# Token-major branch gates and unsplit first blocks in a three-layer float32 network

## The chip, the cores and the metric

One core of a Trainium2 chip runs the whole program in one launch. The metric is the device time of that launch in microseconds (us); lower is better. The times shown are the median of several runs; one more execution was profiled, and every duration below is of that execution.

## What is computed

A sequence of 256 tokens with 2048 features goes through three layers in float32, one after the other.

```python
# first_block: attention, retention and memory branches, then
x = x + rms_norm(mixed @ w_out, g_post_mix)
h2 = rms_norm(x, g_pre_ffn)
f_gate, f_up = split(h2 @ w_ffn_in)                  # feed-forward
x = x + rms_norm((silu(f_gate) * f_up) @ w_ffn_out, g_post_ffn)
# second_block, layer 0: state-space mixer
h = modulate(rmsnorm(x, norm_g[0]), shift, scale)
u, z = split(h @ w_in)
...
x = x + gate * ((y * sigmoid(y @ w_glu + b_glu)) * silu(z) @ w_out)
# second_block, layer 1: attention with three branches
h_kv = modulate(rmsnorm(x, kv_norm_g), kv_shift, kv_scale)
kv = h_kv @ w_kv
proj = h @ w_qg                                      # queries, gates, z
o_br = stack([o_cmp, o_sel, o_win])
o = sum(gates * silu(z) * o_br)                      # over the 3 branches
x = x + gate * (o @ w_o)
out = rmsnorm(x, final_norm_g)
```

The precision has to be that of float32. The kernel gets it by writing each operand as a sum of two parts, hi and lo, of the type float32r, and adding three products: hi hi, hi lo and lo hi.

## The kernel before

**Weights.** A weight matrix is read in units of 2 contraction steps (of 128 rows) by 512 columns, 512 KB. `unit` (line 169) loads one into a tile `raw` (four buffers) from SP's queue and lets `split` (line 148) write `hi` by a cast on ACT (line 156) and `lo` by a subtraction (line 157) on DVE, or on POOL where an engine is given. Three buffers each hold `whi` and `wlo`.

**Products.** `ws` (line 190) makes a feature-major block: the weights are stationary, the 256 tokens move, 24 products of 256 columns a unit. `as_` (line 224) makes a token-major block: 128 tokens of the operand are stationary, 512 weight columns move, 12 products of 512 columns a unit. Both go over the units once and have both token halves in each. After each unit `pump` takes steps of side work (tables of the state-space layer, modulation vectors, attention) into the same queues. `do_late` runs steps that a block left for the middle of the next one.

**By halves.** Where a layer's output must be complete before the next layer's norm, the last block is made by token halves: `as_last` (line 277) keeps the split units in slots (`by_tokens`, line 254) and runs all units for tokens 0 to 127, then for 128 to 255, so that the first half's norm can run under the second half's products. `as_first` (line 301) does the same for the first block of the next layer: all units of the first half, then of the second, with split weights (eight units; subtractions on POOL by `shared=True`) and `ready(k, t)` called one unit ahead, which turns two feature blocks of half `t` on PE, scales them and splits them. The turning product multiplies by a diagonal of the reciprocal norms (`diags`, line 355), made by a chain of small DVE instructions (`rstd` and `rstds`, lines 326 to 374) behind sums of squares on ACT (`square`, line 343).

**The three first blocks.** The feed-forward's first block (line 915) is an `as_` with `ahead(ready)`, where `ready` is that of `post_norm` (line 842); the state-space layer (`ssm`, from line 1376) and the attention layer (`nsa`, from line 1696) call `as_first`, their operands made by `ssm_operand` (line 1345) and `nsa_operand` (line 1666). `hold` and `hold_act` put the splits of the first block's weights behind the first half's diagonal on DVE and the last square on ACT.

**The gate blocks.** In `nsa` each of four head groups makes three blocks of 512 columns of `w_qg` (one a branch) with `ws`, applies silu, multiplies by the branch's attention output, adds the branches up feature-major in `acc` and splits the sum into the operand `o`. `nsa_attention` makes the outputs feature-major, with one product of 512 columns (4 heads x 128 tokens) for a block of keys.

**The order of the work.** Each engine has one queue with a fixed order, found at build time by a scheduler that simulates the program; `issue_after(ins)` puts what is issued inside it behind `ins` on the engine of `ins`.

Of the kernel before, what the change touches and what calls it, by code (L numbers as in the profile page):

```python
# [64 lines left out]

class Slot:
# [7 lines left out]
class Kernel:  # L74
# [8 lines left out]
    def __init__(self, tc, a, out, ctx):  # L83
# [10 lines left out]
        self.hold = self.hold_act = None  # L94
# [74 lines left out]
    def unit(self, wv, k0, c0, n=512, j=None, place=None, engine=None):  # L169
# [9 lines left out]
        rows = wv[:, k0:k0 + 2] if len(wv.shape) == 3 else wv[:, k0 // 4, k0 % 4:k0 % 4 + 2]  # L179
        nc.sync.dma_start(raw[:, :, :n], rows[:, :, c0:c0 + n])  # L180
# [9 lines left out]
    def ws(self, act, wv, c0, j=None, before=None, quiet=False, shared=False):  # L190
# [6 lines left out]
        for k0 in range(0, nk, 2):  # L197
            if before is not None:
                before(k0)
            hi, lo = self.unit(wv, k0, c0, j=j, engine=self.nc.gpsimd if shared else None)  # L200
            for n in range(4):
                c = slice(n * 128, n * 128 + 128)
                for k in range(2):
                    self.mm3(ps[n // 2][:, n % 2], hi[:, k, c], lo[:, k, c], act, k0 + k,
                             start=k0 + k == 0 and n % 2 == 0, stop=k0 + k == nk - 1)
            if before is None and not quiet:
                self.pump()
        return ps
# [15 lines left out]
    def as_(self, act, wv, c0, before=None, quiet=False, shared=False):  # L224
# [6 lines left out]
        for k0 in range(0, nk, 2):  # L231
# [4 lines left out]
            hi, lo = self.unit(wv, k0, c0, engine=self.nc.gpsimd if shared else None)  # L236
# [17 lines left out]
    def by_tokens(self, units, products, shared=False, beside=None):  # L254

# [5 lines left out]
        for t in range(2):  # L261
            for u, (wv, k0, c0) in enumerate(units):
                if t == 0:
                    place = self.slot([128, 2, 2, 512], F32R, "kept") if u < len(units) - 3 else None
                    with self.tc.issue_after(self.hold) if self.hold else nullcontext(), \
                            self.tc.issue_after(self.hold_act) if self.hold_act else nullcontext():
                        kept.append((place, self.unit(wv, k0, c0, place=place,
                                                      engine=self.nc.gpsimd if shared else None)))
# [4 lines left out]
                if t and beside:  # L273
                    beside.popleft()()
# [26 lines left out]
    def as_first(self, act, wv, c0, ready):  # L301


        units = [(wv, k0, c0) for k0 in range(0, 16, 2)]
        ps = [self.mp.tile([128, 512], F32, name=f"mm{i}") for i in range(2)]

        def products(t, u, hi, lo):
            r = slice(t * 128, t * 128 + 128)
            if u == 0:
                ready(0, t)  # L310
            if u < 7:
                ready(u * 2 + 2, t)
            for k in range(2):
                kk = u * 2 + k
                xh, xl = act.hi(kk)[:, r], act.lo(kk)[:, r]
                self.mm(ps[t], xh, hi[:, k], kk == 0, False)
                self.mm(ps[t], xh, lo[:, k], False, False)
                self.mm(ps[t], xl, hi[:, k], False, kk == 15)

        self.by_tokens(units, products, True)  # L320
        self.hold = self.hold_act = None
        return ps
# [518 lines left out]
    def post_norm(self, act, w, g, x_src):  # L841
# [8 lines left out]
        h2 = Act(self, 0)  # L850
        r, beside = [], deque()
# [6 lines left out]
        def done(t, b, p):  # L858
            add(t, b, p)
            r.append(self.rstds(ss[:, t:t + 1]))  # L860
            if t == 0:
                for i in range(4):
                    normed(i, 0)
                for k in range(0, 16, 4):
                    beside.append(partial(both, k))
# [6 lines left out]
        def both(k):  # L872
            ready(k, 0)
            ready(k + 2, 0)

        def ready(k, t):

            while h2.n < k + 2:
                h2.grow()
            if t == 1 and k % 4 == 0:  # L880

                with self.tc.issue_after(self.last_scaled) if k else nullcontext():
                    normed(k // 4, 1)
            elif t == 1:
                with self.tc.issue_after(self.last_hi):
                    for i in range(2):
                        self.square(xs[i].t[:, k // 4 * 512:k // 4 * 512 + 512], new[:, i, k // 4:k // 4 + 1])
            p = self.ps([128, 2, 128], "tp", 2)
            rows = slice(t * 128, t * 128 + 128)
            for j in range(2):  # L890
                nc.tensor.transpose(p[:, j], xs[t].t[:, (k + j) * 128:(k + j) * 128 + 128], self.ident)
            for j in range(2):
                self.split(h2.hi(k + j)[:, rows], h2.lo(k + j)[:, rows], p[:, j], self.vec["g_pre_ffn"][:, k + j:k + j + 1])
# [10 lines left out]
        return xs, h2, partial(ready, t=1), new  # L904

    def ffn(self, xs, h2, ready, ss):
# [5 lines left out]
        for f0, f1 in ((0, 3), (3, 6), (6, 9), (9, 11)):  # L912
            s = Act(self, (f1 - f0) * 4)
            for f in range(f0, f1):
                ps = self.as_(h2, wi, f * 512, before=None if f else self.ahead(ready), shared=f == 0)
# [35 lines left out]
            for b in range(2 if last else 4):  # L951
                ps = self.as_(s, wo[:, f0 * 4:f1 * 4], b * 512)
# [9 lines left out]
        def done(t, b, p):  # L962
            with self.tc.issue_after(self.hold) if self.hold else nullcontext():
# [4 lines left out]
            for i in range(4):  # L968
# [3 lines left out]
                last_square = self.square(x, new[:, t, i:i + 1])  # L972
            ds.extend(self.diags(new[:, t:t + 1]))
            if t == 0:
                self.hold, self.hold_act = self.last_diag, last_square
                for k in range(0, 4, 2):
                    operand[1](k, 0)

        self.as_last(s, wo[:, 36:], (2, 3), done)
# [26 lines left out]
    def first(self):  # L1006
# [57 lines left out]
        xs, h2, ready, ss = self.post_norm(mx, a["w_out"], a["g_post_mix"], a["x"][0])  # L1064
# [3 lines left out]
        operand = self.ffn(xs, h2, ready, ss)  # L1068
# [278 lines left out]
    def ssm_operand(self, xs, ds):  # L1347
# [3 lines left out]
        h = Act(self, 0)  # L1351
        there = set()

        def ready(k, t):
# [3 lines left out]
            while h.n < k + 2:  # L1358
                h.grow()
            p = self.ps([128, 2, 128], "tp", 2)  # L1360
            w = self.work([128, 2, 128], "half")
# [3 lines left out]
            for j in range(2):  # L1365
                c = slice(k + j, k + j + 1)
# [623 lines left out]
```

## Time and profile before

| | us |
|---|---|
| median of 3 runs | 3202.23 |
| lowest, highest | 3200.45, 3205.97 |
| the profiled execution | 3202.57 |
| its span, first to last instruction | 3200.7 |

In the profile PE is the matmul part of TensorE, PEld its weight loads, DVE VectorE, ACT ScalarE, POOL GpSimd, SP the queue that issues most loads. A plain float32 product stands as two records, one of float32r as one. The granted clock of TensorE is given as a share of its full speed, and has two levels here, 1.00 (2.4 GHz) and 0.50 (1.2 GHz).

### The profile page before, as it was taken

What the parts mean: (1) busy time and instruction counts of PE and PEld (TensorE: products, weight loads), DVE (VectorE), ACT (ScalarE), POOL (GpSimd) and SP (SyncE); (2) the same over time, 40 slices, a digit from 0 to 9 for tenths busy, and PEclk for the clock granted to TensorE, in tenths of its full rate; (3) what the DMA queues carried; (4) which work ended last, traced back from release to release, by engine and by line L of the source; (5) the groups of instructions that cost most, each with busy time, mean ns of one, the idle gap of its engine ahead of it and who ended that gap; (6) DMA issues with size and microseconds to landing.
All of it is one profiled execution on the core that took longest, in us unless ns stands there. A gap on an engine that the chain in (4) does not pass through costs nothing. (4 is left out here: it accounts for less than half of the span.)

```text
span 3200.7 us, 48551 instructions
## 1 busy us (share of the span) xinstructions
PE 3108.7 (97%) x18694; PEld 2684.0 (84%) x18694; DVE 2344.8 (73%) x3580; ACT 1461.7 (46%) x2066; POOL 204.8 (6%) x296
## 2 busy tenths in 40 slices
PE   9999999999999998999999999799999899999998
PEld 8999888988888886877878778678898798999997
DVE  7777787767887766999989956656577865655656
ACT  5544444344444445444334355455444534444544
POOL 0000000000000002000000045400000200000000
PEclk9999999999999999999999999899999999999999
DMA  8868867888778874787777799388888585455575
GB/s 281 262 193 271 256 213 232 257 280 272 230 247 271 262 269 153 236 277 248 260 260 264 264 324 331 122 262 284 233 242 266 168 276 156 139 152 158 148 234 165
DMA packets 428040, 753.43 MB, mean 235 GB/s; under 512 B 31764, under 2 KB 90808, under 8 KB 426912
## 3 DMA queue, kind: packets, MB, share of 16 engines
q1 hardware_dynamic: 413520, 710.39, 69.6%
q0 software_dynamic: 13648, 38.88, 3.5%
q8 instruction: 146, 2.39, 0.3%
q10 hardware_dynamic: 640, 1.07, 0.1%
q14 instruction: 86, 0.70, 0.1%
HBM read 725.13 MB, written 33.49 MB: 237 GB/s over the span
## 5 line engine op out<-in xcount | busy, mean ns | idle before, releaser
L156 ACT CAST whi<-raw 128x1024 fp32r<-128x1024 f32 (+2 forms) x1059 | 1030.4, 982 | 1326.2 <-PE mm L150 1137.0
L157 DVE TENSOR_TENSOR wlo<-raw,whi 128x1024 fp32r<-128x1024 f32 (+2 forms) x1045 | 1178.2, 1136 | 585.0 <-ACT whi L156 574.3
L150 PE MATMUL mm<-whi,act 128*128 128x512 f32 x5072 | 1586.8, 392 | 6.4 <-ACT whi L156 5.6
L150 PEld LDWEIGHTS mm<-whi,act 128*128 128x128 f32 x5072 | 952.3, 188 | 214.8 <-issue 10.2
L150 PE MATMUL mm<-act,whi 128*128 128x256 f32 (+1 forms) x5440 | 1010.7, 287 | 3.9 <-ACT whi L156 3.8
L150 PE MATMUL mm<-wlo,act 128*128 128x512 f32 x2536 | 996.5, 393 | 13.8 <-DVE wlo L157 11.8
L150 PEld LDWEIGHTS mm<-act,whi 128*128 128x128 f32 (+1 forms) x5440 | 850.7, 192 | 27.2 <-issue 18.5
L150 PE MATMUL mm<-act,wlo 128*128 128x256 f32 (+1 forms) x2720 | 776.3, 288 | 2.5 <-DVE wlo L157 2.5
L150 PEld LDWEIGHTS mm<-wlo,act 128*128 128x128 f32 x2536 | 477.4, 188 | 125.4 <-DVE wlo L157 21.3
L150 PEld LDWEIGHTS mm<-act,wlo 128*128 128x128 f32 (+1 forms) x2720 | 519.2, 192 | 15.6 <-issue 10.1
L1097 DVE SCALAR_TENSOR_TENSOR acc<-side_raw,c_act,acc 128x512 f32<-128x512 f32 x480 | 359.2, 748 | 18.8 <-DMA side_raw<-mod_w 14.1
L150 PE MATMUL mm<-kept,act 128*128 128x512 f32 x360 | 93.1, 404 | 7.7 <-DVE act L157 7.7
L150 PEld LDWEIGHTS mm<-kept,act 128*128 128x128 f32 x360 | 68.3, 194 | 22.9 <-DVE act L157 8.8
L1117 POOL DMA_DIRECT2D mod<-side x24 | 12.0, 500 | 940.7 <-ACT side L1116 939.1
L1315 POOL DMA_DIRECT2D direct<-kern x128 | 66.9, 544 | 27.6 <-DMA direct<-kern 16.6
L1285 DVE TENSOR_TENSOR side<-tables,ssm_c 128x512 f32<-128x512 f32 x64 | 65.5, 1082 | 3.7 <-DMA ssm_c<-ssm_c_re 3.7
L150 PE MATMUL tp<-diag,x 128*128 128x128 f32 x192 | 32.0, 313 | 21.8 <-DVE diag L363 15.7
L150 PEld LDWEIGHTS tp<-diag,x 128*128 128x128 f32 x192 | 30.5, 224 | 26.2 <-issue 9.0
L156 ACT CAST kept<-raw 128x1024 fp32r<-128x1024 f32 x30 | 31.2, 1049 | 32.9 <-DMA raw<-w_out 8.2
L160 DVE SCALAR_TENSOR_TENSOR act<-tp,vec,act 128x256 fp32r<-128x256 f32 (+1 forms) x64 | 25.4, 412 | 22.1 <-ACT act L159 22.0
L157 DVE TENSOR_TENSOR kept<-raw,kept 128x1024 fp32r<-128x1024 f32 x20 | 24.5, 1225 | 21.0 <-ACT kept L156 20.8
L346 ACT ACTIVATE big<-x 128x512 f32<-128x512 f32 x40 | 25.1, 629 | 28.1 <-DVE x L1653 18.8
(390 smaller groups left out, 1889.5 us busy)
## 6 DMA issues: line engine op xcount, KB each, us to landing
raw<-w_in SPq DMA_DIRECT2D x272, 512.0 KB, 4.5
side_raw<-mod_w SPq DMA_DIRECT2D x192, 512.0 KB, 5.3
raw<-w_ffn_in SPq DMA_DIRECT2D x176, 512.0 KB, 5.3
raw<-nsa_w_qg SPq DMA_DIRECT2D x128, 512.0 KB, 3.7
raw<-w_ffn_out SPq DMA_DIRECT2D x88, 512.0 KB, 6.0
side_raw<-kv_mod_w SPq DMA_DIRECT2D x64, 512.0 KB, 4.7
raw<-ssm_w_in SPq DMA_DIRECT2D x64, 512.0 KB, 5.4
raw<-w_kv SPq DMA_DIRECT2D x48, 512.0 KB, 4.0
```

The source lines that it names most:

```text
L150: return self.nc.tensor.matmul(out, lhsT, rhs, start=start, stop=stop, skip_group_check=True).ins
L156: self.last_hi = nc.scalar.copy(hi, src).ins
L157: self.last = (engine or nc.vector).tensor_sub(lo, src, hi.bitcast(F32)).ins
L160: self.last_scaled = nc.vector.scalar_tensor_tensor(lo, src, scale, hi.bitcast(F32), op0=OP.mult, op1=OP.subtract).ins
L346: return self.nc.scalar.activation(self.work([128, 512], "big"), x, AF.Square, accum_out=out).ins
L1097: nc.vector.scalar_tensor_tensor(acc, raw[:, k], c, acc, op0=OP.mult, op1=OP.add)
L1117: nc.gpsimd.dma_start(flat[n:n + 4].rearrange("(o k) p -> o (k p)", o=1), row[r])
L1285: nc.vector.tensor_mul(w[i], y[r][:, :, :, None].to_broadcast([128, 4, 8, 16]), x[q][:, :, None, :].to_broadcast([128, 4, 8, 16]))
L1315: nc.gpsimd.dma_start(self.direct[g // 8, :, g % 8].rearrange("(c s) w -> c s w", s=8), src)
```

## The change

**Unsplit first blocks.** A class `Unsplit` holds an operand as plain float32 in two slots. The three `ready` functions write the scaled operand there and no longer split it. `as_first` takes the weights as they are loaded (six units in three slots, two in `raw` buffers), with one plain float32 product in place of three, and no weight is split. While the second half's products run, `rest(k)` splits the operand, two contraction steps of both halves at a time, for the later blocks. The feed-forward's first block becomes an `as_first` too; its first-half operand is made beside the second half of the last block of `post_norm`, as are two steps in the other two layers, by `beside(u)`.

**The queue behind the operand's splits.** When the fifth of these eight splits has been issued, `hold` remembers its two instructions, and the next `as_` issues the splits of its units 0 to 2 behind them. `hold_act` and the POOL engine for subtractions are gone. The feed-forward's last `as_` takes no side work.

**Token-major gates.** The twelve gate blocks use `as_`; the attention outputs are made token-major, four products of 128 columns for one of 512; the sum over branches is transposed and split for each group by `transpose_act`, as late work of the next block. `ws` runs late work after its second unit.

```diff
+class Unsplit:
+    def x(self, i):
+        while len(self.slots) <= i // 8:
+            self.slots.append(self.k.slot([128, 8, S], F32, "unsplit"))
+        return self.slots[i // 8].t[:, i % 8]
+    def rest(self, act):
+        def rest(k):
+            while act.n < k + 2:
+                act.grow()
+            self.k.split(act.hi(k, 2), act.lo(k, 2), self.slots[k // 8].t[:, k % 8:k % 8 + 2])
...
 ws:
+            if k0 == 2:
+                self.do_late()
...
 as_:
-            hi, lo = self.unit(wv, k0, c0, engine=self.nc.gpsimd if shared else None)
+            with ExitStack() as held:
+                for ins in self.hold:
+                    held.enter_context(self.tc.issue_after(ins))
+                hi, lo = self.unit(wv, k0, c0)
+            if k0 == 4:
+                self.hold = ()
...
-    def as_first(self, act, wv, c0, ready):
+    def as_first(self, x, wv, c0, ready, rest):
+        for t in range(2):
             r = slice(t * 128, t * 128 + 128)
+            ready(0, t)
+            for u in range(8):
+                k0 = u * 2
+                if u < 7:
+                    ready(k0 + 2, t)
+                if t == 0:
+                    if u < 6:
+                        if u % 2 == 0:
+                            slots.append(self.slot([128, 2, 2, 512], F32, "kept_raw"))
+                        raw = slots[-1].t[:, u % 2]
+                    else:
+                        raw = self.wp.tile([128, 2, 512], F32, name="raw", bufs=4)
+                    self.nc.sync.dma_start(raw, self.rows_of(wv, k0)[:, :, c0:c0 + 512])
+                    raws.append(raw)
+                for k in range(2):
+                    self.mm(ps[t], x(k0 + k)[:, r], raws[u][:, k], k0 + k == 0, k0 + k == 15)
+                if t:
+                    rest(k0)
+                    if u == 4:
+                        self.hold = self.last, self.last_hi
...
 post_norm:
+        def beside(u):
+            if u > 3:
+                ready(u * 2 - 8, 0)
...
 ffn:
-                ps = self.as_(h2, wi, f * 512, before=None if f else self.ahead(ready), shared=f == 0)
+                ps = self.as_(h2, wi, f * 512) if f else self.as_first(first[0], wi, 0, *first[1:])
...
-                ps = self.as_(s, wo[:, f0 * 4:f1 * 4], b * 512)
+                ps = self.as_(s, wo[:, f0 * 4:f1 * 4], b * 512, quiet=last and b == 1)
...
-            with self.tc.issue_after(self.hold) if self.hold else nullcontext():
+            with self.tc.issue_after(self.last_diag) if t else nullcontext():
                 add(t, b, p)
...
 nsa:
-                ps = self.ws(h, wq, D + 48 + br * D + g * 512)
+                ps = self.as_(h, wq, D + 48 + br * D + g * 512)
...
+            self.late += [partial(self.transpose_act, [acc[:, t] for t in range(2)], o, 4, g * 4, 0.5), self.Q[g].free]
...
 nsa_attention:
-                    self.mm(o.rearrange("p h t -> p (h t)"), self.vsw.t[:, br, m, g * 128:g * 128 + 128],
-                            pT.rearrange("p h t -> p (h t)"), m == 0, m == t)
+                    for h in range(4):
+                        self.mm(o[:, h], pT[:, h], self.vsw.t[:, br, m, g * 128:g * 128 + 128], m == 0 and h == 0, m == t)
```

## Rows read from the trace of the kernel before

**Rows 1.** The page, first part: busy us, share, instructions of each engine.
```profile
PE 3108.7 (97%) x18694; PEld 2684.0 (84%) x18694; DVE 2344.8 (73%) x3580; ACT 1461.7 (46%) x2066; POOL 204.8 (6%) x296
```

**Rows 2.** Stretches: from:to, length, busy per engine (instructions), PE clock, DMA share, GB/s.
```profile
1226.00:1261.00 35.00, 27.06 (x115) 19.30 (x114) 22.83 (x59) 20.16 (x52) 15.54 (x7) 0.95 0.42 119
2012.00:2070.00 58.00, 36.73 (x160) 31.05 (x161) 40.77 (x76) 27.14 (x55) 26.18 (x19) 0.76 0.29 88
2489.00:2507.00 18.00, 9.88 (x44) 7.48 (x43) 16.96 (x30) 7.93 (x18) 12.49 (x7) 0.81 0.77 253
2800.00:2840.00 40.00, 40.00 (x317) 37.98 (x315) 20.76 (x26) 20.06 (x29) 0.00 (x0) 1.00 0.54 158
```

**Rows 3.** Stretches of PE alone: from:to, length, busy, clock, DMA share, GB/s.
```profile
1237.09:1240.50 3.41, 3.41 (x9) 0.50 0.00 0
2015.33:2035.81 20.48, 9.63 (x36) 0.50 0.37 113
2046.05:2052.87 6.82, 4.92 (x17) 0.50 0.49 149
2500.02:2506.85 6.83, 3.07 (x10) 0.50 0.71 218
```

**Rows 4.** Timeline of PE from 2011: start, us, instruction, idle before and its releaser.
```profile
2011.51 0.39 PE L150 MATMUL mm<-whi,act 128*128 128x512 f32 x1
2020.52 2.05 PE L150 MATMUL tp<-diag,x 128*128 128x128 f32 x8 [8.63 <-DVE diag L363]
...
2047.95 2.07 PE L150 MATMUL tp<-diag,x 128*128 128x128 f32 x8 [7.09 <-DVE diag L363]
```

**Rows 5.** Timeline of DVE and POOL there, from the first half's last addition on.
```profile
2004.45 0.69 DVE L946 TENSOR_TENSOR y<-mm,y 128x512 f32<-128x512 f32 x1 [3.58 <-PE mm L150]
2013.46 2.17 POOL L1315 DMA_DIRECT2D direct<-kern  x4
2013.86 0.16 DVE L341 SCALAR_TENSOR_TENSOR bit<-bit 128x1 f32<-128x1 f32 x1
2014.06 6.32 DVE L363 TENSOR_SCALAR diag<-ident,bit 128x128 f32<-128x128 f32 x1
2015.53 4.75 POOL L157 TENSOR_TENSOR kept<-raw,kept 128x1024 fp32r<-128x1024 f32 x2
2506.21 0.28 DVE L363 TENSOR_SCALAR diag<-ident,bit 128x128 f32<-128x128 f32 x1
```

**Rows 6.** Line 157 on POOL: count, ns least, median and most, first and last start.
```profile
L157 POOL TENSOR_TENSOR wlo<-raw,whi x14: 2332/2390/2817, 1222.6 to 2500.2; 128x1024 fp32r<-128x1024 f32 x14
```

**Rows 7.** Timeline of PE: runs of equal products; x is how many a row merges.
```profile
1213.78 6.28 PE L150 MATMUL mm<-kept,act 128*128 128x512 f32 x27
...
1290.21 0.60 PE L807 MATMUL tp<-ident,big 128*128 128x128 f32 x4
...
2065.15 1.05 PE L150 MATMUL tp<-diag,x 128*128 128x128 f32 x8
...
2710.89 1.02 PE L150 MATMUL pv<-side,vsw 128*128 128x512 f32 x2
...
2711.98 0.28 PE L150 MATMUL mm<-act,wlo 128*128 128x256 f32 x1
...
2970.19 0.40 PE L150 MATMUL mm<-act,whi 128*128 128x256 f32 x2
```

**Rows 8.** Groups by line: ACT in 2012 to 2070, one PE: count, busy us, mean ns, idle.
```profile
L1371 ACT ACTIVATE half<-tp,mods 128x128 f32<-128x128 f32 x16 | 7.2, 455 | 14.0 <-PE tp L150 14.0
L156 ACT CAST kept<-raw 128x1024 fp32r<-128x1024 f32 x5 | 4.9, 1039 | 0.0
L346 ACT ACTIVATE big<-x 128x512 f32<-128x512 f32 x4 | 2.5, 626 | 1.4 <-DVE x L971 1.4
...
L150 PE MATMUL pv<-side,vsw 128*128 128x512 f32 x48 | 24.6, 592 | 0.0
```

**Rows 9.** Issues of loads: queue, count, KB each, median us to landing.
```profile
raw<-w_ffn_in SPq DMA_DIRECT2D x176, 512.0 KB, 5.3
```

## What the change should do, told before the run

> **What bounds the kernel now.** I read the page's first part first: PE is busy for 3108.7 of 3200.7 us and no other engine comes near it [rows 1]. So time is saved in two ways only: PE work becomes shorter, or PE's idle or slowly clocked stretches are filled. I then took the busy time by stretches. In an ordinary stretch of the gate blocks PE is busy all the time at full clock; in three short stretches elsewhere it is not: 27.06 of 35 us, 36.73 of 58 us and 9.88 of 18 us [rows 2]. These are the three first blocks that the change rewrites (feed-forward, state-space layer, attention layer; below stages A, B and C). Idle there is 7.9, 21.3 and 8.1 us. Four stretches inside them ran at a granted clock of 0.50, the lower of the two levels, with PE busy for 3.41, 9.63, 4.92 and 3.07 us [rows 3]; half of that is lost: 1.7, 7.3 and 1.5 us. Together the stages lose 9.6 + 28.6 + 9.6 = 47.8 us. That is all there is to win in them.
>
> Why PE waits there is read in stage B in the order of time. PE's last product starts at 2011.51; the next work, turning token half 0, starts at 2020.52 and waited 8.63 us for the diagonal on DVE; the second half's waited 7.09 us for its own [rows 4]. That diagonal took 6.32 us from 2014.06, where its fellow needs 0.28; all that time POOL worked, from 2015.53 on at weight subtractions (L157) [rows 5]. By the code `shared=True` puts eight such subtractions a stage on POOL, of 2.4 us each [rows 6]. So the gaps are mostly a norm chain on DVE that POOL holds up, with the weight casts on ACT held behind it.
>
> **Part 1, unsplit first blocks: the products.** Each of the three stages has 2 halves x 16 contraction steps = 32 places where three split products become one product of plain float32. A run of 27 split products of 512 columns takes 6.28 us, one alone 0.39, so one comes every (6.28 - 0.39) / 26 = 0.227 us, three 0.68 [rows 4, 7]. A plain product is not in these stages, but of the same shape in attention: it runs as two records whose starts lie 1.02 - 0.59 = 0.43 us apart, so 0.86 [rows 7, 8]. Price: 32 x (0.86 - 0.68) = 5.8 us a stage, **+17.3 us** in three. The turns and transposes stay as many as they were.
>
> **Part 1, what it gives back.** Eight weight casts on ACT (1.04 us each [rows 8]) and eight subtractions on POOL go from each stage, and with them the stretching of DVE. What stays, by stage:
> - Stage B. The first half's chain is as before up to 2014.06, then 0.28 for the diagonal: PE idles 2.5 us instead of 8.6, then turns a first pair and waits for one scale on ACT (0.46 us [rows 8]), say 0.6 us. The clock may still fall: after the other long gaps it was low for 6.82 and 6.83 us [rows 3], so between 0 and 3.4 us are lost; I take 3.4. The second half's chain then runs under the first half's products, 16 x 0.86 = 13.8 us plus 32 turning records at (1.05 - 0.60) / 4 = 0.11 (eight against four small records [rows 7]), 17.3 in all, from about 2015.7 to 2033. The first half's chain took from 2004.45 (addition) to 2014.06, 9.6 us [rows 5]; starting at about 2015.0, with eight scales on DVE between, taken at ACT's 0.46, it ends near 2028, so 5 us of cover are left. Should the cover go, each us of chain is a us of PE. Left: 6.5 us.
> - Stages A and C. The first half's operands are there before the products of the stage before have ended (they are turned beside the last units), so PE goes straight on. The second half has 14 to 17 us of cover as in B. Left: nothing but the seam below.
> - The seam, in all three. `rest` splits the operand eight times a stage (ACT about 0.6, DVE about 0.7, by the instructions of 128x512 [rows 5, 8]); it hides under the second half's products. Behind the fifth of these splits the next block's units 0 to 2 are queued on ACT and DVE. From there four units of products, 4 x 1.72 = 6.9 us, remain; ACT has three operand splits and three casts, 1.8 + 3.1 = 4.9 us, DVE 2.1 + 3.7 = 5.8: covered, and PE, which waits for the first of them, needs only unit 0. The loads are tighter: the last two of the eight raw tiles stand in the four-buffer pool and are read by PE until the second half's last two units, so the next block's third unit can be asked for 1.7 us before the end, lands 5.3 us later and is cast at +4.6 [rows 8, 9]; PE wants it at 2 x 2.72 = +5.4. Nothing to 1 us; I take 1 us a stage. SP issues in order, so a load that waits there holds up the side work's loads as well, which PE does not wait for at once.
> Left in all: 6.5 + 3 = 9.5 us; recovered 47.8 - 9.5 = **38.3 us**.
>
> The shared port is the place for a rule against this. In the row the diagonal began while POOL still issued DMAs (four until 2015.63) and ended only with the subtractions behind them [rows 5]; a one-column instruction just before it took 0.16 us beside the same DMAs, so I let it end at 2014.34. The Trainium skill, page SBUF — State Buffer, section "Who interferes with whom", says that VectorE's tensor_scalar on SBUF data can take a port pair that it shares with GpSimd, and that whichever issues first holds it for the whole instruction. By it the DMAs alone would hold the diagonal until 2015.63, and the sum would be 1.3 us larger. No row here separates DMAs from subtractions.
>
> **Part 2, token-major gates.** 12 blocks x 8 units = 96 units change from 24 products of 256 columns to 12 of 512. The short ones come every 0.40 - 0.28 = 0.12 us [rows 7]: 2.88 us a unit against 12 x 0.227 = 2.72. 96 x 0.16 = **-15.5 us**, and PE is busy throughout there [rows 2], so it counts in full. Added: eight transposes for each of four groups, 32 at 0.11 = 3.6 us. The 32 products with the probabilities become four of 128 columns each: eight records at 0.11, 0.88 to 0.90 against 0.86, so 0.6 to 1.3 us in all, I take 1.0 (the turning records, also with a fresh stationary tile each, are the nearest; fewer records cannot make it a gain). The last group's transposes come inside the output product and are needed only at its seventh unit. Sum **-10.9 us**. Loads must come a little faster, 512 KB per 2.72 us = 193 GB/s; stage C had 253 [rows 2].
>
> **Part 3, order.** The four units without side work at the feed-forward's end push a few steps behind it, into a stage with idle engines: nothing, at most the 1 to 2 us that one more group of POOL DMAs may cost the second half's chain, which has cover. Moving the slots and `issue_after`s costs nothing; the addition of half 1 stays behind the first diagonal as before.
>
> **Sum.** -38.3 + 17.3 - 10.9 = -31.9 us against the profiled execution's own 3202.57 us (span 3200.7, 1.9 around it), which stands 0.3 above the median of the three runs: 3170.7, so **3171 us**. Bounds: with no slow clock and no seam 3164; with 2 us more at each seam, the first diagonal held until POOL's DMAs end at 2015.63 (1.3 us [rows 5]) and the loads of half 0 at 253 GB/s [rows 2] (eight tiles in 16.6 us where A wants 15.3) 3180.
>
> **Rivals.**
> 1. The seam becomes the new wait. If all loads of the next block waited for the end of half 1, its first product comes 5.3 + 1.04 = 6.3 us late, 5.3 more than allowed: three times, 3187. For it: two of four raw tiles held by PE; against: the other two are free early and no side loads are asked for meanwhile.
> 2. The second half's chain stays late in B: its small steps share DVE, in a fixed order, with the first half's scales, and it waited 7.09 us before [rows 4]; against it, the cover of 5 us and POOL's absence. If so, the 7.1 us and some 1.5 of slow clock remain: 3179.
> 3. Gates bring nothing. In the rows the long products cost 0.227 and the short ones 0.12, so both carry about the same 0.013 over their columns and halving their number saves it; should spacing follow columns alone, the 15.5 us vanish and 4.6 are added: 3186. The Trainium skill, page TensorE: Matmul & The Clock Gate, section "Back-to-back issue gap", gives N/2.4 + 2.5 ns, so 109 and 216: it would leave 3 us of the saving, 3183. The rows speak against it.
> 4. The change doesn't do what it says: the order found for the queues leaves the gaps half filled, so that 24 us come back and the dearer products eat them: about 3185 to 3202.
> 5. Slower. ACT and DVE become the bound in the first blocks: operand splits and next splits go before half 1's own operands, the gaps stay whole and the seam of rival 1 is added: 3202.6 + 17.3 + 15.9 - 10.9 = 3225. It decides once less than 22.3 of the 47.8 us come back. Against it: ACT is busy for only 27 of 58 us in B [rows 2] and loses 8.3 us of casts.
>
> **How the numbers follow.** Forecast 0.65 (own range 3164 to 3180), rival 1 0.13, rival 2 0.07, rival 3 0.03, rival 4 0.05 (half of it within 0.2%), rival 5 0.07. A measurement of this kernel tells about 0.2% (6.4 us) from no change. Faster 0.65 + 0.13 + 0.07 + 0.03 + 0.02 = 0.90, same 0.03, slower 0.07. The range takes in rivals 1 to 3 and 6 us under the lower bound, because the order of all queues is found anew for the changed program and gaps outside the stages may move as well: 3158 to 3189.
>
> **What would show it.** No tensor instruction on POOL from L157, and both diagonals in B at 0.3 us. In B the time from PE's last feed-forward product to the stage's end falls from 58 to about 42 us, with one gap of 2 to 4 us; A and C show no PE gap over 1 us before the seam. Plain products come every 0.43 us a record. Gate units take 2.72 us. I am wrong if gaps ended by `whi` or `wlo` appear behind the first blocks (rival 1), if the second half again waits for its diagonal (rival 2), or if half 1's scales wait in ACT's queue (rival 5).

## The result, and the profile after

The changed kernel takes **3167.8 us** (median of four, 3164.8 to 3175.0) beside 3202.0 for the kernel before: ratio 0.9895, 95% interval 0.9876 to 0.9913, so 28 to 40 us less. Forecast were 3171 and a range of 3158 to 3189. The profiled execution is the longest of the four, 3174.97 us with a span of 3173.2; its sums are made against the 3200.7 of the trace before.

The busy line of the page after, to be read beside [rows 1]: PE 3 us busier, in a span that is 27.5 us shorter, and POOL 57.5 us less busy.

```profile
PE 3111.7 (98%) x17670; PEld 2626.5 (83%) x17670; DVE 2310.8 (73%) x3556; ACT 1434.8 (45%) x2018; POOL 147.3 (5%) x272
```

The windows of stages A, B and the start of C, then one slowly clocked stretch (columns as in [rows 2]). Idle there is 0, 4.65 and 1.35 us, where [rows 2] have 7.9, 21.3 and 8.1:

```profile
1224.00:1262.00 38.00, 38.00 (x130) 21.16 (x129) 25.90 (x78) 21.50 (x49) 0.00 (x0) 1.00 0.28 87
2005.50:2070.00 64.50, 59.85 (x224) 38.58 (x224) 37.75 (x76) 27.34 (x49) 8.27 (x13) 0.95 0.38 120
2465.00:2485.00 20.00, 18.65 (x75) 11.51 (x75) 11.44 (x30) 6.17 (x13) 0.54 (x1) 1.00 0.80 286
2010.87:2017.70 6.83, 5.44 (x10) 2.86 (x11) 4.56 (x15) 1.73 (x5) 0.61 (x1) 0.50 0.00 0
```

The timeline of PE after, one row from A, then B from its last feed-forward product on (to be read beside [rows 4]; x is how many records a row merges):

```profile
1245.44 1.88 PE L173 MATMUL mm<-kept_raw,unsplit 128*128 128x512 f32 x4
...
2005.17 0.39 PE L173 MATMUL mm<-whi,act 128*128 128x512 f32 x1
2006.78 1.13 PE L173 MATMUL tp<-diag,x 128*128 128x128 f32 x8 [1.23 <-DVE diag L405]
2009.06 1.12 PE L173 MATMUL mm<-kept_raw,unsplit 128*128 128x512 f32 x2 [1.15 <-ACT unsplit L1409]
2012.26 2.07 PE L173 MATMUL mm<-kept_raw,unsplit 128*128 128x512 f32 x2 [2.07 <-DVE unsplit L1407]
...
2030.58 1.05 PE L173 MATMUL tp<-diag,x 128*128 128x128 f32 x8
2031.84 1.98 PE L173 MATMUL mm<-kept_raw,unsplit 128*128 128x512 f32 x4 [0.20 <-ACT unsplit L1409]
```

The wait of 8.63 us for the first diagonal is 1.23, and the 7.09 for the second is gone: half 1 begins to turn at 2030.58 without waiting. The third wait, 2.07, is new. DVE and POOL show where it comes from:

```profile
2004.83 4.16 POOL L1357 DMA_DIRECT2D direct<-kern  x8 [1.05 <-DMA direct<-kern]
2006.35 0.29 DVE L405 TENSOR_SCALAR diag<-ident,bit 128x128 f32<-128x128 f32 x1
2008.69 2.82 DVE L415 SCALAR_TENSOR_TENSOR bit<-bit 128x1 f32<-128x1 f32 x1 [0.27 <-ACT big L388]
2008.93 2.55 POOL L990 TENSOR_TENSOR y<-y,gb 128x512 f32<-128x512 f32 x2
2011.80 0.40 DVE L1407 TENSOR_SCALAR unsplit<-tp,mods 128x128 f32<-128x128 f32 x1
```

The diagonal took 0.29 us in the middle of eight POOL DMAs. Later a one-column instruction, 0.16 us elsewhere, took 2.82 and ended with POOL's last product of y and gb; the scale that PE waits for stands behind it in DVE's queue.

**A table by stage.** For each kernel I took the start of the same five instructions in its trace and subtracted the start in the trace before (1351.8, 2093.0, 2487.7, 2655.4 and the span's end, 3200.7). The columns are the differences from one mark to the next, in us, less is faster: A to the first of the two tanh of the third feed-forward block, B to the last of the four writes of u behind the first two ssm blocks, the ssm layer's side work to C's first turn, C to the first copy of q, and from there to the end. The right column is the median time; all kernels of the table come up below. A sum is that of one profiled execution and stands some us beside the medians.

| kernel | A | B | side work | C | q to end | sum | median us |
|---|---|---|---|---|---|---|---|
| changed kernel | -5.7 | -15.9 | +1.7 | +0.5 | -8.1 | -27.5 | 3167.8 |
| e1: gates alone | -0.8 | -1.6 | -6.0 | +1.0 | -8.3 | -15.7 | 3187.2 |
| e2: first blocks alone | -6.7 | -17.0 | +3.9 | -4.3 | -0.1 | -24.2 | 3178.6 |
| e3: before, subtractions on DVE | -1.4 | -13.7 | -1.2 | -3.3 | 0.0 | -19.6 | 3181.5 |
| e4: changed, without the order | -3.5 | -10.3 | -1.0 | -2.3 | -8.2 | -25.3 | 3179.0 |
| e5: changed, y*gb on DVE | -6.7 | -19.1 | -3.0 | -3.6 | -8.0 | -40.4 | 3162.3 |
| e6: changed, A split | -3.2 | -18.3 | -0.8 | -3.5 | -8.2 | -34.0 | 3170.4 |
| e7: changed, C split | -7.8 | -17.6 | +3.1 | -3.5 | -8.2 | -34.0 | 3168.8 |
| e8: changed, B split | -7.4 | -12.7 | -4.4 | -3.5 | -8.2 | -36.2 | 3169.8 |
| e9: before, three small edits | -1.6 | -17.2 | -7.8 | -1.4 | -8.3 | -36.3 | 3168.1 |
| e10: changed, idle work on POOL | -0.3 | -2.1 | -2.9 | +2.0 | -8.1 | -11.4 | 3193.6 |
| e11: changed, A, B and C split, y*gb on DVE | -2.5 | -17.4 | -4.2 | -1.9 | -8.1 | -34.1 | 3165.9 |
| e12: e5, state steps later | -6.1 | -20.3 | +11.4 | -4.5 | -8.1 | -27.6 | 3174.8 |

Two columns tell how to read the rest. From q to the end all kernels with the new gates agree within 0.3 us, and those without them stand at 0: that number is firm. The side work wanders from -7.8 to +3.9 (e12, which edits it, left out), and by -6.0 in e1, whose edit does not touch it: differences there of some us are not the edit's. The order of the queues, which is found anew for each program, is the likely cause; executions of one program differ too (3164.8 to 3175.0 for the changed kernel, of which the table has the slowest).

### The profile page after: what moved, and what is told of

Its sections match the earlier page's. It is cut to its first block, busy times and chain, and to the rows that moved or that the text cites. A ratio compares the mean times of both kernels' runs of the same rounds, so it can differ in the third digit from the quotient of the medians.

```text
span 3173.2 us, 46364 instructions
## 1 busy us (share of the span) xinstructions
PE 3111.7 (98%) x17670; PEld 2626.5 (83%) x17670; DVE 2310.8 (73%) x3556; ACT 1434.8 (45%) x2018; POOL 147.3 (5%) x272
## 5 line engine op out<-in xcount | busy, mean ns | idle before, releaser
L173 PE MATMUL mm<-whi,act 128*128 128x512 f32 x5728 | 1796.3, 393 | 7.7 <-ACT whi L179 7.7
L173 PEld LDWEIGHTS mm<-whi,act 128*128 128x128 f32 x5728 | 1075.2, 188 | 242.8 <-issue 13.4
L173 PE MATMUL mm<-wlo,act 128*128 128x512 f32 x2864 | 1129.9, 395 | 9.6 <-DVE wlo L180 9.6
L173 PE MATMUL mm<-act,whi 128*128 128x256 f32 x3904 | 726.0, 287 | 3.7 <-ACT whi L179 3.7
L173 PEld LDWEIGHTS mm<-wlo,act 128*128 128x128 f32 x2864 | 539.1, 188 | 133.2 <-DVE wlo L180 17.7
L173 PEld LDWEIGHTS mm<-act,whi 128*128 128x128 f32 x3904 | 612.4, 193 | 18.5 <-issue 10.7
L173 PE MATMUL mm<-act,wlo 128*128 128x256 f32 x1952 | 554.2, 287 | 2.3 <-DVE wlo L180 2.2
L173 PEld LDWEIGHTS mm<-act,wlo 128*128 128x128 f32 x1952 | 374.1, 193 | 7.8 <-DVE wlo L180 4.2
L173 PE MATMUL mm<-kept_raw,unsplit 128*128 128x512 f32 x144 | 71.5, 615 | 4.8 <-DVE unsplit L1407 2.1
L1357 POOL DMA_DIRECT2D direct<-kern x128 | 66.9, 539 | 26.0 <-DMA direct<-kern 15.7
L173 PE MATMUL mm<-kept,act 128*128 128x512 f32 x240 | 57.6, 390 | 0.0
L173 PEld LDWEIGHTS mm<-kept_raw,unsplit 128*128 128x128 f32 x144 | 25.3, 196 | 23.1 <-issue 12.5
L173 PEld LDWEIGHTS tp<-diag,x 128*128 128x128 f32 x192 | 27.4, 194 | 15.9 <-issue 15.1
L180 DVE TENSOR_TENSOR kept<-raw,kept 128x1024 fp32r<-128x1024 f32 x20 | 24.5, 1224 | 19.7 <-ACT kept L179 19.6
```

Of the source, the lines that this page charges most:

```text
L173: return self.nc.tensor.matmul(out, lhsT, rhs, start=start, stop=stop, skip_group_check=True).ins
L180: self.last = (engine or nc.vector).tensor_sub(lo, src, hi.bitcast(F32)).ins
L1357: nc.gpsimd.dma_start(self.direct[g // 8, :, g % 8].rearrange("(c s) w -> c s w", s=8), src)
```

## The experiments

The theory: the gaps of the first blocks are a norm chain on DVE that POOL's tensor instructions hold up; with them gone, and with operands that need no split, PE goes on. The main rival: the unsplit operands alone make the gain, by relieving ACT and DVE, and POOL has nothing to do with it.

**e1, e2: the two halves of the change.** e1 takes the gates' hunks alone on the kernel before, e2 all the others.

> The kernel before with the token-major gates alone; its first blocks stay split. Theory (the forecast's second part): 96 gate units go from 2.88 to 2.72 us and 4.6 us are added, so 10.9 us less than the kernel before, 3191 us beside its 3202. Rival (spacing follows columns alone): no saving and 4.6 us more, 3207. By the traces of the whole change, whose gate blocks came 8 us nearer to the start, 3194. Gate units of 2.72 us in the trace speak for the theory, of 2.88 for the rival.

> The kernel before with the unsplit first blocks and their order alone; its gates stay feature-major. Theory (the forecast's first part): 38.3 us of the stages' 47.8 come back and 17.3 us are paid for plain products, 21.0 less: 3181. By the whole change's 34 us less the forecast of the gates: 23 less, 3179. If the two parts help each other (a rival), both runs together fall short of 34 us by more than 6: this one above 3185.

e1: 3187.2 beside 3200.8, ratio 0.9961 (0.9949 to 0.9973), so 9 to 16 us less. e2: 3178.6, ratio 0.9927 (0.9914 to 0.9940), 19 to 28 less. The middles, 12.5 and 23.4, add to 36; the whole change has 34, so the parts do not help each other. By the table 8.3 of e1's gain is the gates' own.

**e3: the kernel before, with its weight subtractions on DVE.**

```
-        self.by_tokens(units, products, True)
+        self.by_tokens(units, products)
...
-   ps = self.as_(h2, wi, f * 512, before=None if f else self.ahead(ready), shared=f == 0)
+   ps = self.as_(h2, wi, f * 512, before=None if f else self.ahead(ready), shared=False)
```

> The kernel before with one edit: the 24 weight subtractions of the first blocks go to DVE instead of POOL; operands stay split, no plain product, gates as before. Rival (POOL alone made the gaps): the diagonals take 0.3 us, all gaps close as they did in the whole change, and without the 17.3 us for plain products that is 38 us less, 3164. Theory (the operands' own splits and casts are the other half): the diagonals do take 0.3 us, about 6 us a diagonal come back in the ssm block, but DVE has 8 subtractions of 1.2 us more a stage and the halves still wait for their splits in the feed-forward block: 6 to 14 us less, 3188 to 3196.

3181.5 us, ratio 0.9936 (0.9924 to 0.9947): 17 to 24 less. That lies between theory and rival of its text: more than the theory gave (6 to 14) and less than the rival's 38. With operands still split, two words bring most of what e2 brings. DVE and PE in its stage B:

```profile
2014.39 0.29 DVE L363 TENSOR_SCALAR diag<-ident,bit 128x128 f32<-128x128 f32 x1
2014.60 1.28 DVE L946 TENSOR_TENSOR y<-mm,y 128x512 f32<-128x512 f32 x2
2015.79 6.75 DVE L157 TENSOR_TENSOR kept<-raw,kept 128x1024 fp32r<-128x1024 f32 x4
...
2014.83 1.13 PE L150 MATMUL tp<-diag,x 128*128 128x128 f32 x8 [2.60 <-DVE diag L363]
2022.99 1.43 PE L150 MATMUL tp<-diag,x 128*128 128x128 f32 x5 [7.03 <-DVE half L1368]
```

The diagonal is short again. What remains, 7.03 us, is four weight subtractions in DVE's queue ahead of the first scaled half; two of them ran beside y*gb on POOL and took 2.29 and 2.28 us, not 1.22. This rest is what unsplit operands take away in B: -15.9 to -17.0 against -13.7.

**e4: the changed kernel without its third part.**

```
-            with ExitStack() as held:
-                for ins in self.hold:
-                    held.enter_context(self.tc.issue_after(ins))
-                hi, lo = self.unit(wv, k0, c0)
-            if k0 == 4:
-                self.hold = ()
+            hi, lo = self.unit(wv, k0, c0)
```

> The changed kernel without its third part: the splits of the next three weight units are no longer queued behind the unsplit operand's own splits. Theory: the order costs and brings little, since PE is fed either way: 3165 to 3172. Rival (it is needed): casts and subtractions of the next block go ahead of the second half's operands, which then wait up to 4.9 us of ACT in each of three stages: up to 3183, with PE gaps ended by unsplit in the second halves.

3179.0 us, ratio 0.9931 (0.9919 to 0.9943), 11 us behind the changed kernel: the rival holds, and not quite by its way. PE, DVE and ACT of its stage B:

```profile
2018.54 1.84 PE L173 MATMUL tp<-diag,x 128*128 128x128 f32 x7 [10.53 <-DVE diag L400]
...
2006.42 2.59 DVE L180 TENSOR_TENSOR wlo<-raw,whi 128x1024 fp32r<-128x1024 f32 x2 [1.86 <-ACT whi L179]
2012.63 1.23 DVE L180 TENSOR_TENSOR wlo<-raw,whi 128x1024 fp32r<-128x1024 f32 x1 [2.17 <-ACT whi L179]
2018.11 0.29 DVE L400 TENSOR_SCALAR diag<-ident,bit 128x128 f32<-128x128 f32 x1
...
2011.56 1.04 ACT L179 CAST whi<-raw 128x1024 fp32r<-128x1024 f32 x1 [3.80 <-DMA raw<-ssm_w_in]
```

The next block's three subtractions stand ahead of the first half's diagonal in DVE's queue. The third waits for a cast, the cast for its load, and so the norm chain waits for a load it does not need. The order is no trimming: it is a condition of the unsplit blocks.

**e5: the changed kernel, with y*gb on DVE.**

```
-                    (nc.gpsimd if b > 1 else nc.vector).tensor_mul(yc, yc, gb.t[:, c])
+                    nc.vector.tensor_mul(yc, yc, gb.t[:, c])
```

> The changed kernel with one edit: the two products y*gb that POOL still does ahead of the ssm block go to DVE. Theory (a one-column DVE instruction is held for as long as POOL's tensor instructions run): no DVE instruction of 0.16 us near the first half's diagonal takes longer than 0.5, the gap of 2.07 us before the first products falls under 1, two additions of 1.3 us in all lie on DVE's chain of the second half, which has cover; with the slow clock behind it 2 to 5 us less than the changed kernel, 3163 to 3166. Rival (the instruction waited for something else, POOL's DMAs or ACT): the stretch of 2.8 us stays and the time is 3168 or, with 1.3 us more on the chain, 3169.

**3162.3 us**, ratio 0.9875 (0.9861 to 0.9888), the fastest kernel here; beside 0.9895 (0.9876 to 0.9913) the gain of 6 us over the changed kernel is not sure by these intervals alone. The mechanism is: no DVE instruction is stretched there any more. Of the 12.9 us between the two sums of the table B has 3.2; the rest stands in columns that the edit does not touch, most of it in the side work and C. DVE and PE of its stage B:

```profile
2007.88 0.29 DVE L405 TENSOR_SCALAR diag<-ident,bit 128x128 f32<-128x128 f32 x1
2011.59 0.16 DVE L415 SCALAR_TENSOR_TENSOR bit<-bit 128x1 f32<-128x1 f32 x1
...
2008.32 1.13 PE L173 MATMUL tp<-diag,x 128*128 128x128 f32 x8 [1.90 <-DVE diag L405]
2009.98 1.98 PE L173 MATMUL mm<-kept_raw,unsplit 128*128 128x512 f32 x4 [0.54 <-ACT unsplit L1409]
2011.80 0.61 PE L173 MATMUL tp<-diag,x 128*128 128x128 f32 x4
```

**e6, e7, e8: one block split again.** Each puts one of the three first blocks back to split weights and operand, with the subtractions on DVE and all of half 0 ahead of half 1 (`as_split` holds the products that `as_first` had in the kernel before, without `shared`). The edit of e6, those of e7 (C) and e8 (B) alike:

```
-                o, g = unsplit.x(k + j)[:, t * 128:t * 128 + 128], self.vec["g_pre_ffn"][:, k + j:k + j + 1]
...
+                self.split(h2.hi(k + j)[:, rows], h2.lo(k + j)[:, rows], p[:, j], self.vec["g_pre_ffn"][:, k + j:k + j + 1])
...
-   ps = self.as_(h2, wi, f * 512) if f else self.as_first(first[0], wi, 0, *first[1:])
+   ps = self.as_(h2, wi, f * 512) if f else self.as_split(h2, wi, 0, first)
```

> The changed kernel with the feed-forward's first block split again (weights and operand, subtractions on DVE), but in the changed order: all of half 0, then all of half 1. Theory (the block gained 7 us by the order of its halves and by POOL's absence, and unsplit products cost it 5.8): no PE gap over 1 us in the block and 5 to 6 us less than the changed kernel, 3162 to 3163. Rival (the unsplit operand is what closes the gaps): with 8 casts of 1.04 us and 8 subtractions of 1.2 us more in the block, half 1 waits for its operands, 5 to 8 us of gaps come back and the time is 3167 to 3171.

> The changed kernel with the attention layer's first block split again, subtractions on DVE. The kernel before with its subtractions on DVE had gaps of 3.9 us here instead of 8.1, and plain products cost 5.8. Theory (the block gets no more from unsplit products than it pays): 2 to 4 us less than the changed kernel, 3164 to 3166. Rival: the gaps of 4 us and the seam return whole and the time is the same or 2 us more, 3168 to 3170.

> The changed kernel with the ssm layer's first block split again, subtractions on DVE. The kernel before with its subtractions on DVE had gaps of 2.60 and 7.03 us here, the second ended by a half that stood behind weight subtractions on DVE. Theory (this is the block where casts and subtractions stand in the way of the norm chain, so unsplit products pay): 7 us of gap and about 2 of slow clock return and 5.8 are saved, 2 to 5 us more than the changed kernel, 3170 to 3173. Rival (POOL's subtractions were all of it here too): 4 to 6 us less, 3162 to 3164.

3170.4, 3168.8 and 3169.8 us, ratios 0.9900, 0.9898 and 0.9899, with intervals of 0.0014 to 0.0017 to either side: none can be told from the changed kernel. So the gains of 5 and 2 to 4 us that e6's and e7's theories gave do not show, and e8 lies 0.2 us under the range of its theory, too near to the changed kernel to bear it out. By the table unsplit operands are worth 3 to 5 us in A (-3.2 split, -5.7 to -7.8 not), 3 to 6 in B (-12.7 split, -15.9 to -18.3 not), and nothing in C, where e7 has -3.5 as the unsplit kernels have. e6's window of A shows why the split block is no faster for its cheaper products: 4.6 us idle, and a clock of 0.91.

```profile
1224.00:1262.00 38.00, 33.41 (x139) 24.11 (x138) 26.58 (x81) 23.67 (x58) 0.00 (x0) 0.91 0.36 115
```

These edits undo two things at once: `as_split` sets no `hold`, so the block that goes back to split weights also loses the order of the queue, which the kernel before had in B and C. In B of e8 PE waits 10.60 us for the first diagonal, with weight subtractions ahead of it on DVE, in e11 (below) 7.41; in e3, whose old order stands, it waits 2.60. So the 3 to 6 us in B are not the price of split operands alone.

```profile
2015.82 2.05 PE L173 MATMUL tp<-diag,x 128*128 128x128 f32 x8 [7.41 <-DVE diag L425]
```

**e9, e11: all of it without unsplit operands.** e9 is the kernel before with the edits shown for e1, e3 and e5; e11 is e5 with the edits of e6, e7 and e8.

> The kernel before with three edits: token-major gates, the first blocks' weight subtractions on DVE, the products y*gb on DVE. No unsplit block, old order of halves. Theory (POOL's tensor instructions were the cause, and unsplit products bring no more than their 17.3 us of price): the single runs add up, 20 for the subtractions, 12 for the gates, 5 for y*gb, less what overlaps: 3163 to 3168, as fast as the changed kernel or a little faster. Rival (the unsplit blocks carry a gain of their own beside it): 3172 or more.

> The changed kernel's order with all three first blocks split again, subtractions and y*gb on DVE, so no tensor instruction on POOL there. Theory (unsplit or split makes little difference once POOL is out): the three single undoings gave -1 to +2 us each; with y*gb on DVE 3162 to 3167. Rival (they only looked free one at a time, since a loss in one block was made up in the side work behind it): above 3172.

e9: 3168.1, ratio 0.9897 (0.9884 to 0.9911). e11: 3165.9, ratio 0.9888 (0.9875 to 0.9902). Both theories hold (e9 at the upper end of its range): with POOL's tensor instructions out of the way and the gates turned, a kernel without any unsplit block is as fast as the changed one.

**e10: the changed kernel, with idle work on POOL.** Added is a subtraction of each of the first six weight tiles of a block from itself, whose result nobody reads (no load of the block waits for these six tiles).

```
                     raws.append(raw)
+                    if u < 6:
+                        self.nc.gpsimd.tensor_sub(idle.t[:, u % 2], raw, raw)
```

> The changed kernel with idle work put back on POOL: in each first block six subtractions of 128x1024 of the weight tiles whose result nobody reads. Theory (POOL's tensor instructions hold DVE's, whoever needs their result): one-column DVE instructions of the norm chain are stretched to 2 to 6 us again, PE gaps ended by DVE return in the ssm and attention blocks, 8 to 20 us more than the changed kernel: 3176 to 3188. Rival (the gaps of before came from waiting for POOL's results): nobody waits for these, so 3166 to 3170.

3193.6 us, ratio 0.9983 (0.9974 to 0.9992): 26 us behind the changed kernel, more than forecast. Eighteen instructions whose results nobody reads take back three quarters of the whole gain, so the gaps were no wait for POOL's results. DVE, POOL and PE in its stage B:

```profile
2017.01 8.30 DVE L420 SCALAR_TENSOR_TENSOR bit<-bit 128x1 f32<-128x1 f32 x1 [0.27 <-ACT big L393]
2017.14 2.61 POOL L995 TENSOR_TENSOR y<-y,gb 128x512 f32<-128x512 f32 x2
2019.58 5.70 POOL L355 TENSOR_TENSOR idle<-kept_raw 128x1024 f32<-128x1024 f32 x3
...
2026.06 1.22 PE L173 MATMUL mm<-kept_raw,unsplit 128*128 128x512 f32 x1 [6.61 <-DVE unsplit L1412]
```

One column on DVE takes 8.30 us and ends 0.03 us after the last of five POOL instructions that follow each other without a break (2019.58 + 5.70 = 2025.28).

**e12: what is late next.** In e5 PE still idles 6.79 us at 2079, because ACT's queue holds a copy of u, which waits 9.03 us for its way through memory, ahead of three weight casts.

```
-        for _ in range(4):
+        for _ in range(6 if q0 else 7):
             yield self.side[0][1]
```

> The changed kernel with y*gb on DVE and one more edit, behind the ssm block: the first state steps start seven weight units after the values u are written, not four, and the second ones six, not four. In the trace with y*gb on DVE alone PE idled 6.79 us at 2079.46 because ACT's queue held the copy of u, which waited 9.03 us for its round trip through memory, ahead of three weight casts, and 3.39 us at 2143.58 for the same round trip. Theory (this is where part of the gain goes back, and only the place in the queue makes it): both gaps fall under 1 us and 8 to 13 us are gained on 3162, 3150 to 3155. Rival (the chain of states behind it then ends too late): the gaps move to the scan and the direct part, 3160 to 3166.

3174.8 us, ratio 0.9916 (0.9903 to 0.9929): slower than e5 by 12, and outside the ranges of theory and rival, a miss. ACT, first in e5, then in e12:

```profile
2081.43 3.82 ACT L1529 COPY u_group<-u_chunk 64x1024 f32<-64x1024 f32 x2 [9.03 <-DMA u_chunk<-u]
2085.15 2.95 ACT L179 CAST whi<-raw 128x1024 fp32r<-128x1024 f32 x3
```

```profile
2081.84 3.78 ACT L1529 COPY u_group<-u_chunk 64x1024 f32<-64x1024 f32 x2 [9.68 <-DMA u_chunk<-u]
2085.53 2.94 ACT L179 CAST whi<-raw 128x1024 fp32r<-128x1024 f32 x3
```

The copy did not move in ACT's queue though it is written three units later; PE idles 7.39 us in the same place. The state steps behind it did come later, and the side work pays 14 us more than in e5. An explicit order, as the change has for the splits, was not tried.

## Why the prediction was right

**Point by point.** The sum -20.9 for the first blocks came out as -23.4 in e2, the -10.9 for the gates as -8.1 in the table. The first blocks gave 2.5 us more and the gates 2.8 less; that the time came within 3 us of the forecast is in part luck, since these misses cancel.

- Plain products: right. Four records in a row take 1.88 us, two 1.02, so one comes every 0.43, and a place costs 0.86 as worked out from [rows 7].
- Stage A, forecast -2.8: measured -5.7, and -6.7 in e2. Idle is 0, so the seam of 1 us is not there: PE takes the next block's first units between half 1's plain products. Most of the rest can be restarts. The forecast counted gaps alone, but in a row of products without a gap each takes 0.227 us and the last one its whole 0.39, so each gap costs 0.16 us of busy time beside its idle time; for the ten gaps of over 0.25 us in A of before that is an estimated 1.6. With both, 2.8 becomes 5.4.
- Stage B, forecast -15.3: measured -15.9, and -17.0 in e2. Left over were to be 6.5 us and 1 for the seam. Left over are 1.23 + 1.15 + 2.07 + 0.20 = 4.65 of idle and half of 5.44 at the lower clock, 7.4. The size was right and its make-up not: the first diagonal comes sooner than allowed, and 2.07 come from POOL's y*gb, which the forecast had left among things that stay as they are. The second half's chain was covered, but not by 5 us: its diagonal was ready at 2028.94 and PE turned at 2030.58, 1.6 us later.
- Stage C, forecast -2.8: -4.3 in e2 and -3.6 in e5; the changed kernel's own +0.5 holds a gap of 2.71 us for a load of cmp_w, which is 0.38 in e2's trace; the rest of the difference was not followed. e7 shows that this gain owes nothing to unsplit products.
- Gates, forecast -10.9: -8.1. From the first copy of q to the last q product of DVE 453.6 us became 443.5 (rows below); the last group's transposes and gates then take 2.0 more at the end.

```profile
2655.41 0.59 ACT L1749 COPY q<-mm 128x512 f32<-128x512 f32 x1 [0.51 <-PE mm L150]
3108.98 0.68 DVE L1777 TENSOR_TENSOR q<-q,big 128x512 f32<-128x512 f32 x1
```

```profile
2636.00 0.59 ACT L1783 COPY q<-mm 128x512 f32<-128x512 f32 x1 [0.51 <-PE mm L173]
3079.50 0.68 DVE L1811 TENSOR_TENSOR q<-q,big 128x512 f32<-128x512 f32 x1
```

The products keep their paces, 0.120 and 0.227 us from start to start (medians there), so the saving stands (96 x (24 x 0.120 - 12 x 0.227) = 15.0 for 15.5) and rival 3 falls. The terms against it are 2.3 to 2.8 us larger than 4.6. The likeliest is the products with the probabilities: summed from each start to the next, their 64 records were 23.4 us and the 256 new ones are 29.6, +6.2 where I took +1.0; since a neighbour's time can hide in such a sum, and no run took these products alone, this stays open.

**Part 3 was under-read.** I costed the order at nothing and its absence nowhere. e4 puts its worth at 11 us: the kernel before had a hold of its own, so it is no gain over that one, but without it the unsplit blocks lose half of what they bring. What happens then is near to rival 5, the next block's splits ahead of the block's own operands, but on half 0: the 10.53 us stand ahead of the first diagonal, and not at a seam behind the block. Rival 2 falls with half 1's start, rivals 4 and 5 with the time. Of rival 1 the sign is there and the cause is not: PE waits 7.45 us for `whi`, until 2091.47, 20 us behind the last write of u; the kernel before waits 5.32 there. No load of the block holds it up; the cast stands in ACT's queue behind the copy of u (rows below).

**The shared port.** The forecast weighed whether POOL's DMAs alone would hold the diagonal until 2015.63. In the changed kernel they do not: 0.29 us among eight of them. Tensor instructions do, and the trace shows more than the forecast drew from [rows 5]: the held instruction can start ahead of POOL's (0.13 us in e10, 0.24 after, 1.47 before) and still end with the last of POOL's back-to-back run. In these three POOL was issuing DMAs when it started, and the tensor instructions stood behind them in POOL's queue. Where POOL's instruction was itself still waiting, DVE's went through: in e3 the first of the four subtractions starts 0.97 us ahead of y*gb, which waits 0.79 us for ACT, and takes its usual 1.21. Nor is it always the whole run: in the kernel before a one-column instruction that starts at 2022.44, inside the first of two such products, ends with that first one after 0.71 us, though the next follows without a break. What decides between the two no run shows. The Trainium skill, page SBUF — State Buffer, section "Who interferes with whom", says that a VectorE instruction with two SBUF inputs contends with a GpSimd instruction that reads SBUF, and that whichever issues first gets the shared ports. The first half agrees with e10. The second agrees with e3; with the three held instructions it agrees only if POOL's instruction had issued before the start that the trace gives it, which no run shows.

**What the forecast had right for a partly wrong reason.** Its views named POOL's subtractions as the cause of the gaps, and e3 and e10 bear that out. But the sum credited the recovery to the rewriting of the blocks. Two words in e3 recover 20.5 us without paying the 17.3 for plain products; of the whole rewriting, unsplit operands are worth 3 to 5 us in A and, up to the mark, 2 in B (with y*gb on DVE -19.1 against -17.4 and -17.2 split), after their price, and nothing in C. What B has is given back right behind its mark. The copy of u there waits longer where B is unsplit (ACT of before, after and e8, then PE of after):

```profile
2106.17 3.81 ACT L1492 COPY u_group<-u_chunk 64x1024 f32<-64x1024 f32 x2 [7.58 <-DMA u_chunk<-u]
2086.66 3.81 ACT L1529 COPY u_group<-u_chunk 64x1024 f32<-64x1024 f32 x2 [9.71 <-DMA u_chunk<-u]
2084.39 4.05 ACT L1553 COPY u_group<-u_chunk 64x1024 f32<-64x1024 f32 x2 [5.93 <-DMA u_chunk<-u]
2091.47 1.22 PE L173 MATMUL mm<-whi,act 128*128 128x512 f32 x2 [7.45 <-ACT whi L179]
```

From the last write of u to the end of PE's gap there it is 19.1 to 22.2 us in the eight kernels with an unsplit B and 15.2 to 18.3 in the six with a split one. Taken from A's mark to that end, e8 is 14.1 us ahead of the kernel before and the changed kernel 13.7; e11 is 18.4 ahead, e9 20.0 and e5 18.0. So in the time nothing is left of what unsplit operands win in B; why the wait grows was not followed.

The question that the profile of before could have answered, and that I did not ask it, is what the gaps would be with the subtractions on DVE alone.

## What to carry to other kernels

When a tiny DVE instruction takes microseconds, look at what POOL runs when it ends, and take POOL's tensor instructions out of that stretch first: a word or two here brought most of what a rewriting brought. Before a rewriting is credited, cost the smallest edit that removes the same cause, and put the mark up to which its gain is counted behind the next wait: 2 us won in B were lost again within 20. And an order in the queues is part of an edit: leaving it out cost 11 us (e4), and moving a step in the source moved nothing in ACT's queue (e12).

## What the runs showed of the hardware

- A one-column DVE instruction (0.16 us) can be held for a whole chain of POOL tensor instructions, up to 8.30 us (e10), though nobody needs most of their results; another ended with the first of two (0.71 us, before). POOL's DMA issues beside a 128x128 DVE instruction cost it nothing (0.29, after).
- A product takes 0.39 us alone and 0.227 in a row, so by estimate a gap costs 0.16 us beside its idle time: many small gaps cost more than their idle time.
- With 4.6 us idle of 38 the granted clock of A's window was 0.91 (e6), without any it was 1.00 (the changed kernel, e5). In the kernel before it was 0.95 with 7.9 idle of 35, so the idle time alone does not set it.
